# Scores' low-half products of two heads side by side on 64 rows each, the softmax of two heads at once, a permuted identity for the position adds, and the first loads spread over two queues

## The chip, the core and the metric

The kernel runs on one core of one Trainium2 chip. The metric is the device time of one execution in microseconds (us). Beside it stands one profiled execution, whose trace is read below. The engines are called as in the profile: PE multiplies matrices, PEld is its loading of weights, DVE, ACT and POOL work on vectors, SP issues most of the transfers.

## The reference

One decoder block on 512 positions of 1024 channels, cut to what the change touches:

```python
h = rms_norm(x, norm_pre)
proj = h @ w_in                       # q, keys and values of three branches, gates, retention, merge gates
# mixer A, 8 heads in 2 groups of 64 channels: compressed, selected and sliding branch
blocks = kv[tok_idx] + pe             # compress_blocks: 32 positions every 16, plus a position term
kc = gelu(flat @ w1) @ w2             # the same for the values
s = einsum('qghd,kgd->qghk', q, k) * scale
p = masked_softmax(s, mask)           # s minus its row maximum, exp, divided by the row's sum
o = g0 * o_cmp + g1 * o_sel + g2 * o_win          # o_branch = p @ v, g = sigmoid(gate)
# mixer B: retention in chunks of 128, 4 heads; then
merged = sigmoid(m_a) * y_a + sigmoid(m_b) * y_b
x = x + rms_norm(merged @ w_out, norm_post)
```

With 512 positions, 8 blocks of 64 and 16 picked blocks, the selected branch sees every earlier position, as the sliding one does, so both are plain causal attention.

## The kernel before

Every product is made of values split in two: a high half of fewer bits and a low half with the rest. A product of two split operands is three matmuls, high by high, low by high, high by low. `hTh` and `hTl` are the two halves of the scaled input, `whi` and `wlo` those of the weights, which stream from memory through four `raw` tiles and are split by ACT or DVE (`splitter`; the high half is a copy, the low half the subtraction that the profile shows as `wlo<-raw,whi`).

PE's order is written by a planner in the kernel (class `Order`): tasks are generators, each operation has an estimated cost, and the planner issues the next instruction of the task that is ready first. The main task is the row of products with the streamed weights; the tails of each product and the attention are spawned tasks that fill in. The order on each engine is fixed when the program is built.

The stages: the first product (`main`, keys and values, eight 128-row slices of the input times four tiles `t` of 128 positions), then the compressed branch's operands and the queries, the hidden layer of the compression, and the other products in the order of `PLAN`, with the attention in between.

- **First loads.** `gp` (the 8 columns of `norm_pre`) comes on ACT's queue, then the first half of the first `raw` tile, also on ACT's queue; SP's queue starts with the first slice of the transposed input (`load_xT(0)`), then the second half of that tile. Eight matmuls with `ident` keep PE busy in the meantime (line 1268). `h_split` (ACT) and `h_low` (DVE) make `hTh` and `hTl`.
- **Position adds.** `tail_a` transposes the keys and values of the compressed branch (line 226, `ident`) and adds the position term while it scatters them into `Xk` and `Xv` (line 201, `arena_f<-bank,cst`, 64 partitions): four adds for each tile `t`, whose innermost run is over 16 positions.
- **Scores.** `qT[t]` holds for each head the high half of the query in 64 rows and the low half in the other 64; `kA` the high half of the keys in both, `kB` their low half in both. One head's scores are two matmuls over all 128 rows:

```python
mm(sv, q, kA[:, b0:b0 + nb, g, 0:L], True, False)
e = mm(sv, q, kB[:, b0:b0 + nb, g, 0:L], False, True)
```

  `L` is 128(t+1), `nb` the number of branches in one task: both for t of 0 and 1, one for 2 and 3. `PS` is a ring of two PSUM banks (`bank2`, `bank3`), one for each head's scores.
- **Softmax.** For each head and branch: mask and row minimum of the negated scores on DVE (line 790, with a read of its accumulator), `Exp` on ACT with the row's sum, the reciprocal on DVE (line 218), and the scaling by reciprocal and gate: on DVE in one instruction (line 210), or on ACT if the planner's clock finds that sooner. `att_unit` and `att_block` then transpose, split and multiply by the values once the four heads of a group are done.

Of the kernel before, what the change touches and what calls it, by code (L numbers as in the profile page):

```python
# [37 lines left out]
WAKE = 8  # L38
# [3 lines left out]
class Order:  # L42
# [5 lines left out]
    def __init__(self):  # L48
        self.now = 0.0
        self.eng = {"act": 0.0, "dve": 0.0, "pool": 0.0, "dma": 0.0}  # L50
        self.ring = 500.0
        self.flying = [0.0] * 8
        self.port = 0.0
        self.exact = False
        self.cos, self.n = [], 0
        self.flags = set()
# [81 lines left out]
def block_kernel(ctx: ExitStack, tc, x, xT, g_pre, ws, small, w2s, norm_post, rope_r, dmask, out):  # L138
# [9 lines left out]
    rp = ctx.enter_context(tc.tile_pool(name="raw", bufs=1))  # L148
    pp = ctx.enter_context(tc.tile_pool(name="ps", bufs=1, space=PSUM))
# [71 lines left out]
    def mm(ps, a, b, start, stop, r=0.0, cost=None):  # L221
        T.matmul(ps, a, b, start=start, stop=stop)  # L222
        return od.pe(cost or max(0.4418 * size(b) + 1, 107 if a.shape[-1] > 64 else 54), r, a.dtype == FT)

    def tr(ps, a, idn, r=0.0):
        T.transpose(ps, a, idn)  # L226
        return od.pe(58 if a.dtype == FR else 107, r, a.dtype == FT)
# [9 lines left out]

    ident = cp.tile([P, P], FT, name="ident")
# [66 lines left out]
    def queue(i, j):  # L305

        return S if i + j == 0 else DMA

    def load_next():
        i = len(raws)  # L310
        if i < len(loads):
            raw = rp.tile([P, 1024], FT, name="raw", tag="raw", bufs=NR)
            o, c, r = loads[i][0], 0, parts[2 * (i - NR) + 1][2] if i >= NR else 0.0
            for j, n in enumerate(loads[i][1]):
                queue(i, j).dma_start(raw[:, c:c + n], ws[o:o + P * n].rearrange("(p n) -> p n", p=P))
                e = od.dma(P * n * 4, r)
                o, c = o + P * n, c + n
            raws.append((raw, e))
# [9 lines left out]
    def splitter():  # L328
        for i, (_, pieces) in enumerate(loads):
            n = sum(pieces)  # L330
            for k in range(2):
# [17 lines left out]
                e = cp_any(vh, src, r)  # L349
# [69 lines left out]
    gp = cp.tile([P, KD], FT, name="gp")  # L419
# [3 lines left out]
    rsrow = bp.tile([P, SEQ], FT, name="rsrow")  # L423
# [3 lines left out]
    def load_xT(k):  # L427
        DMA.dma_start(xTf[k], xT[k * P:(k + 1) * P, :])
        xTr[k] = od.dma(P * SEQ * 4)
# [6 lines left out]
    def h_split():  # L436
        for k in range(KD):
            yield lambda: xTr[k] > 0
            yield xTr[k], "act"
            g = gp[:, k:k + 1]  # L440
            e = act(hTh[:, k, :], xTf[k], r=xTr[k], scale=g)
            od.spawn(h_low(k, e), 0)

    def h_low(k, e):
        yield e, "dve"
        hready[k] = stt(hTl[:, k, :], xTf[k], gp[:, k:k + 1], f(hTh[:, k, :]), OP.mult, OP.subtract, e)
# [89 lines left out]
    def tail_a(t, ps, e, ring):  # L536
# [15 lines left out]
        for i in range(4):  # L552
            ep = tr(pc[:, i * P:(i + 1) * P], kd[:, i * P:(i + 1) * P], ident, e)
        KD6.put(kd, ep)
        yield ep, "dve"
        for i, X in enumerate((Xk, Xv)):
            src = pc[:, i * 256:(i + 1) * 256].rearrange("p (g c l) -> p g c l", g=2, c=8)
            for hf in range(2):
# [132 lines left out]
    def tail_q(t, ps, e):  # L691
# [6 lines left out]
        qs = qT[t].rearrange("p h (s c) -> p h s c", s=2)  # L698
        qv = qn.rearrange("p (h c) -> p h c", h=8)
        e = act(qs[:, :, 0, :], qv, r=e)  # L700
        yield e, "dve"
        e = sub_split(qs[:, :, 1, :], qv, qs[:, :, 0, :], e)
        NAT.put(qn, e)
        for g in range(2):
            pt = yield from PT.get()
            yield e + PE_LAG
            for j in range(4):
                ep = tr(pt.bitcast(FR)[:, j * P:(j + 1) * P],
                        qs[:, g * 4 + j].rearrange("p a b -> p (a b)"), identr, e)
# [65 lines left out]
    def att_head(t, g, brs, j, slot):  # L775

        L, nb, h, b0 = P * (t + 1), len(brs), g * 4 + j, brs[0]
        s = yield from PS.get()
        sv = s[:, 0:nb * L].rearrange("p (b c) -> p b c", b=nb)
        q = qT[t][:, h, :]  # L780
# [4 lines left out]
        Pj = slot["P"]  # L785
        pv = Pj[:, 0:nb * L].rearrange("p (b c) -> p b c", b=nb)
        stat = sp.tile([P, 6], FT, name="stat", tag="stat", bufs=12)
        nm, z, rz = (stat[:, 2 * i:2 * i + 2] for i in range(3))
        for b in range(nb):
            V.tensor_tensor_reduce(pv[:, b, :], sv[:, b, :], maskp[:, 512 - L:512], 1.0, -NEG, OP.add, OP.min,  # L790
                                   nm[:, b:b + 1])
            od.op("dve", 1.04 * L + 80, e)
        e = od.op("dve", 80)
        PS.put(s, e)
        yield e, "act"
        for b in range(nb):
            e = act(pv[:, b, :], pv[:, b, :], AF.Exp, r=e, bias=nm[:, b:b + 1], scale=-1.0, accum_out=z[:, b:b + 1])
        yield e, "dve"
        e = recip(rz[:, 0:nb], z[:, 0:nb], e)
        gc = h * 3 + 1 + b0  # L800
        if max(od.eng["act"], e) + (0.833 * L + 186) * nb + 190 < max(od.eng["dve"], e) + (0.521 * L + 191) * nb:
            e = tt(rz[:, 0:nb], rz[:, 0:nb], gate[:, t, gc:gc + nb], OP.mult, e)
            yield e, "act"
            for b in range(nb):
                e = act(pv[:, b, :], pv[:, b, :], r=e, scale=rz[:, b:b + 1])
        else:
            for b in range(nb):
# [572 lines left out]
```

## Time and profile before

| | |
|---|---|
| time, median of 3 runs | 532.64 us (531.42 to 532.94) |
| the profiled execution's own time | 531.09 us |
| its span, first to last instruction | 529.2 us |
| PE / PEld / DVE / ACT busy | 518.8 / 436.1 / 390.4 / 256.5 us |
| granted TensorE clock, mean | 0.998 |
| matmuls recorded | 2636 |

A matmul's end is modelled in the trace, so its duration holds the tail in which the next one already runs: what PE needs for one is read from the distance of starts, and PE's share of 98% does not say that it never waited. Where PE waited is seen at its weight loads.

### The profile page before, as it was taken

To read this page: it belongs to the slowest core of one execution; us is meant where nothing else is said; L and a number is where in the kernel's file an instruction comes from. 1 tells how busy PE (TensorE), PEld (TensorE's weight loads), DVE (VectorE), ACT (ScalarE), POOL (GpSimd) and SP (SyncE) were. 2 spreads that over 40 slices of the span, in tenths; PEclk is the share of its full clock that TensorE was granted. 3 is DMA by queue.
4 is the path that set the end of the run, shared out by engine and by line. 5 is a ranking of instruction groups with operands and counts; after the bars stand their busy time and mean duration, and the time that the engine had idled before them with its cause. 6 is when DMAs were issued, how large, how long until landed. Compare 5 with 4: busy or idle time off the path is not lost.

```text
span 529.2 us, 7325 instructions
## 1 busy us (share of the span) xinstructions
PE 518.8 (98%) x2636; PEld 436.1 (82%) x2636; DVE 390.4 (74%) x924; ACT 256.5 (48%) x552; POOL 12.9 (2%) x32
## 2 busy tenths in 40 slices
PE   8998999999999999999999999999999999999995
PEld 7896888888788888888888888888888888888885
DVE  6799799899999989997777886777737235345533
ACT  6673589448365785483546253525304224123411
POOL 1000000000000000000010000000000000000000
PEclk9999999999999999999999999999999999999999
DMA  8931127401304013123401441131814033305022
GB/s 327 382 121 54 46 66 239 175 1 40 121 1 130 31 40 117 43 84 115 146 35 41 139 142 58 41 120 40 311 48 159 18 142 125 115 1 159 1 98 101
DMA packets 18131, 55.18 MB, mean 104 GB/s; under 512 B 2096, under 2 KB 3120, under 8 KB 18096
## 3 DMA queue, kind: packets, MB, share of 16 engines
q1 hardware_dynamic: 17808, 54.46, 30.4%
q8 instruction: 20, 0.33, 0.3%
q10 hardware_dynamic: 288, 0.27, 0.2%
q14 instruction: 15, 0.12, 0.1%
HBM read 52.63 MB, written 2.10 MB: 103 GB/s over the span
## 4 chain that ended last, share of the span: by engine, by line
PE 84%; DVE 11%; issue 2%; ACT 2%; DMA 1%; DVEq 0%; POOLq 0%; POOL 0%; ACTq 0%
PE bank L222 79%; PE bank L226 5%; DVE arena_f L201 3%; DVE wlo L201 3%; DVE arena_r L201 2%; DVE arena_f L790 1%; DMA raw<-in_stream_dram 1%; DVE nat L201 1%; ACT arena_r L189 1%; ACT whi L189 1%; DVE arena_f L511 1%; DVE arena_f L210 0%; DVE arena_f L214 0%; ACT nat L189 0%; ACT arena_f L189 0%
## 5 line engine op out<-in xcount | busy, mean ns | idle before, releaser
L189 ACT ACTIVATE whi<-raw 128x512 fp32r<-128x512 f32 x151 | 91.9, 628 | 51.4 <-PE bank L222 42.0
L201 DVE TENSOR_TENSOR wlo<-raw,whi 128x512 fp32r<-128x512 f32 x160 | 102.9, 686 | 3.9 <-ACT whi L189 3.3
L222 PE MATMUL bank<-whi,hTh 128*128 128x512 f32 x256 | 99.4, 404 | 0.9 <-ACT whi L189 0.9
L222 PE MATMUL bank<-wlo,hTh 128*128 128x512 f32 x256 | 96.3, 391 | 0.1
L222 PE MATMUL bank<-whi,hTl 128*128 128x512 f32 x256 | 96.3, 391 | 0.0
L222 PE MATMUL bank<-arena_r 128*128 128x256 f32 (+2 forms) x328 | 70.3, 335 | 0.0
L189 ACT ACTIVATE arena_r<-bank 128x512 fp32r<-128x512 f32 (+2 forms) x80 | 45.1, 570 | 46.5 <-PE bank L226 46.3
L222 PE MATMUL bank<-hTh,whi 128*128 128x512 f32 x160 | 63.4, 396 | 0.0
L222 PE MATMUL bank<-hTh,wlo 128*128 128x512 f32 x160 | 62.6, 391 | 0.2 <-DVE wlo L201 0.2
L222 PE MATMUL bank<-hTl,whi 128*128 128x512 f32 x160 | 62.5, 390 | 0.0
L222 PE MATMUL bank<-arena_r,whi 128*128 128x512 f32 x192 | 59.2, 389 | 0.0
L222 PEld LDWEIGHTS bank<-whi,hTl 128*128 128x128 f32 x256 | 48.1, 188 | 10.5
L222 PEld LDWEIGHTS bank<-arena_r 128*128 128x128 f32 x328 | 50.8, 190 | 6.3 <-DVE stat L790 0.3
L222 PEld LDWEIGHTS bank<-whi,hTh 128*128 128x128 f32 x256 | 48.0, 188 | 9.2 <-ACT whi L189 1.0
L222 PEld LDWEIGHTS bank<-wlo,hTh 128*128 128x128 f32 x256 | 48.2, 188 | 9.0 <-DVE wlo L201 0.5
L201 DVE TENSOR_TENSOR arena_r<-bank,arena_r 128x512 fp32r<-128x512 f32 (+2 forms) x72 | 46.9, 656 | 8.3 <-ACT arena_r L189 7.6
L222 PE MATMUL bank<-whi,arena_r 128*128 128x512 f32 (+1 forms) x176 | 49.0, 353 | 0.0
L222 PEld LDWEIGHTS bank<-arena_r,whi 128*128 128x128 f32 x192 | 36.0, 188 | 7.6 <-DVE sg L214 0.2
L189 ACT ACTIVATE arena_f<-arena_f,stat 128x512 f32<-128x512 f32 (+3 forms) x64 | 35.3, 555 | 11.3 <-DVE stat L790 11.2
L226 PE MATMUL bank<-ident,arena_f 128*128 128x128 f32 (+1 forms) x260 | 38.5, 274 | 1.6 <-DVE arena_f L511 1.0
L226 PEld LDWEIGHTS bank<-ident,arena_f 128*128 128x128 f32 (+1 forms) x260 | 31.0, 138 | 9.9 <-DVE arena_f L511 1.5
L222 PE MATMUL bank<-arena_r,wlo 128*128 128x512 f32 x96 | 37.3, 389 | 0.0
(117 smaller groups left out, 669.6 us busy)
## 6 DMA issues: line engine op xcount, KB each, us to landing
raw<-in_stream_dram SPq DMA_DIRECT2D x79, 512.0 KB, 4.1
arena_f<-in_x_dram SPq DMA_DIRECT2D x8, 512.0 KB, 6.9
arena_f<-in_xT_dram SPq DMA_DIRECT2D x8, 256.0 KB, 5.8
arena_f<-in_rope_r_dram SPq DMA_DIRECT2D x8, 256.0 KB, 2.5
out_dram<-arena_f SPq DMA_DIRECT2D x6, 256.0 KB, 2.0
raw<-in_stream_dram SPq DMA_DIRECT2D x4, 280.0 KB, 7.1
arena_f<-in_norm_post_dram SPq DMA_DIRECT2D x1, 512.0 KB, 7.9
out_dram<-arena_f SPq DMA_DIRECT2D x2, 192.0 KB, 1.9
```

The lines of the kernel that those rows point to most:

```text
L189: S.activation(o, i, func, **kw)
L201: (V if e == "dve" else G).tensor_tensor(o, a, b, op=op)
L222: T.matmul(ps, a, b, start=start, stop=stop)
L226: T.transpose(ps, a, idn)
L511: V.tensor_copy(kd.rearrange("p (a r c) -> p a r c", a=n, r=2), kn[:, a:b].rearrange("p (a c) -> p a c", c=64).unsqueeze(2).broadcast_to([ ...
L790: V.tensor_tensor_reduce(pv[:, b, :], sv[:, b, :], maskp[:, 512 - L:512], 1.0, -NEG, OP.add, OP.min, nm[:, b:b + 1])
```

## The change

- Scores: `att_head` becomes `att_pair`, for two heads. Both heads' first products (`kA`) stay as they are; the second ones (`kB`) use only the 64 rows in which the query's high half stands, rows 0 to 63 for the first head and 64 to 127 for the second. For that, `tail_q` puts the low half first in every second head. The product of the two low halves, which was part of the second matmul, is left out. A pair takes both banks of `PS` at once.
- Softmax: the two heads share `stat`; one reciprocal serves both. The rule that picks the engine for the scaling is another (the sum on ACT's side no longer carries 190, DVE's side gets 1000 more), and on ACT's side one small product of reciprocals and gates goes ahead.
- Positions: the transposes of the compressed branch take `identp`, `ident` with its columns permuted, so that the result stands position by position, and the adds run over 8 or 7 blocks innermost.
- Start: `x0` holds `norm_pre` and the first 256 columns of the first input slice and comes on ACT's queue; SP's queue begins with the first half of the first `raw` tile, then the other 256 columns, then the second half. The first `whi` is always cast by DVE. The matmuls at the start are seven, on a zeroed `rsrow`.
- Planner: other estimated costs for matmuls and transposes.

```diff
-    def pe(self, cost, r=0.0, exact=False):
-        if exact != self.exact:
-            cost += 100.0 if exact else 85.0
-            self.exact = exact
+    def pe(self, cost, r=0.0, after=0.0):
+        cost += 0.0 if after else self.after
+        self.after = after
...
-        return od.pe(cost or max(0.4418 * size(b) + 1, 107 if a.shape[-1] > 64 else 54), r, a.dtype == FT)
+        return od.pe(cost or (0.4418 * size(b) + 2 if size(b) > 64 else 112 if a.shape[-1] > 64 else 54), r)
...
+    identp = ep.tile([P, P], FT, name="identp")
+    V.tensor_copy(identp.rearrange("p (l c) -> p l c", l=16), ident.rearrange("p (c l) -> p l c", l=16))
...
-                e = cp_any(vh, src, r)
+                if p:
+                    e = cp_any(vh, src, r)
+                else:
+                    V.tensor_copy(vh, src)
+                    e = od.op("dve", copy_ns(vh, src), r, True)
...
-            ep = tr(pc[:, i * P:(i + 1) * P], kd[:, i * P:(i + 1) * P], ident, e)
+            ep = tr(pc[:, i * P:(i + 1) * P], kd[:, i * P:(i + 1) * P], identp, e)
...
-                o = X[rr, :, :, c0 + lo:c0 + 8].rearrange("p l g c -> p g c l")
-                ep = tt(o, src[rr, :, lo:8, :],
-                        pes[i][rr, :].unsqueeze(1).unsqueeze(1).broadcast_to([64, 2, 8 - lo, 16]), OP.add, ep)
+                o = X[rr, :, :, c0 + lo:c0 + 8].rearrange("p l g c -> p g l c")
+                ep = tt(o, src[rr, :, :, lo:8],
+                        pes[i][rr, :].unsqueeze(1).unsqueeze(3).broadcast_to([64, 2, 16, 8 - lo]), OP.add, ep)
...
-    def att_head(t, g, brs, j, slot):
-        s = yield from PS.get()
-        mm(sv, q, kA[:, b0:b0 + nb, g, 0:L], True, False)
-        e = mm(sv, q, kB[:, b0:b0 + nb, g, 0:L], False, True)
+    def att_pair(t, g, brs, j, slots):
+        yield lambda: len(PS.free) >= 2
+        for i in range(2):
+            mm(sv[i], qT[t][:, h + i, :], kA[:, b0:b0 + nb, g, 0:L], True, False)
+        for i in range(2):
+            r = slice(i * 64, i * 64 + 64)
+            e = mm(sv[i], qT[t][r, h + i, :], kB[r, b0:b0 + nb, g, 0:L], False, True, cost=15 if i else None)
...
-        if max(od.eng["act"], e) + (0.833 * L + 186) * nb + 190 < max(od.eng["dve"], e) + (0.521 * L + 191) * nb:
+        if max(od.eng["act"], e) + (0.833 * L + 186) * 2 * nb < max(od.eng["dve"], e) + (0.521 * L + 191) * 2 * nb + 1000:
...
-    S.dma_start(gp, g_pre)
-    load_xT(0)
+    S.dma_start(x0, x0s)
     load_next()
...
-        T.matmul(banks[0][:, 0:P], ident, ident, start=True, stop=True)
+        T.matmul(banks[0][:, 0:P], rsrow[:, 0:P], rsrow[:, 0:P], start=True, stop=True)
```

What this makes of the order, at three places. First PE, where the attention of the last tile (t = 3) begins; `bank2` and `bank3` take scores, `bank0` the query product, `identr` marks the transposes of the queries. Before:

```order
L226 MATMUL bank5_86<-identr_94,arena_r_80 128x128 x4
L222 MATMUL bank2_83<-arena_r_80 128x512 x2
L226 MATMUL bank4_85<-identr_94,arena_r_80 128x128 x4
L222 MATMUL bank3_84<-arena_r_80 128x512 x2
L222 MATMUL bank0_81<-whi_414,hTh_98 128x512
L222 MATMUL bank0_81<-wlo_415,hTh_98 128x512
```

After the change:

```order
L222 MATMUL bank2_86<-arena_r_83 128x512
L222 MATMUL bank3_87<-arena_r_83 128x512
L222 MATMUL bank2_86<-arena_r_83 128x512
L222 MATMUL bank3_87<-arena_r_83 128x512
L226 MATMUL bank5_89<-identr_99,arena_r_83 128x128 x4
L222 MATMUL bank0_84<-whi_371,hTh_105 128x512
```

Two heads' four matmuls now stand together, the last two of them on 64 rows each; there are 24 such pairs, 12 with 512 columns, 8 with 384 and 4 with 256. In the program the number of matmuls stays the same but for the one fewer at the start.

Second DVE, at the first scores (line 790 before and 809 after are the masked minimum; the second row of each is the read of its accumulator). Before:

```order
L790 ISA arena_f_79,stat_738<-bank3_84,maskp_113 128x512
L790 ISA stat_738 128x1
L218 RECIPROCAL stat_733<-stat_733 128x1
L210 TENSOR_SCALAR arena_f_79<-arena_f_79,stat_733,gate_115 128x512
L790 ISA arena_f_79,stat_761<-bank2_83,maskp_113 128x512
```

After the change:

```order
L809 ISA arena_f_82,stat_750<-bank3_87,maskp_119 128x512
L809 ISA stat_750 128x1
L218 RECIPROCAL stat_750<-stat_750 128x2
L201 TENSOR_TENSOR stat_750<-stat_750,gate_121 128x2
L809 ISA arena_f_82,stat_771<-bank2_86,maskp_119 128x512
```

The scaling (line 210) is gone from DVE here. In the whole program 58 of the 64 scalings move to ACT (14 of 512 columns, 16 of 384, 16 of 256, 12 of 128), 48 reciprocals become 24, 22 small products with the gates are new, and 7 more copies of `whi` stand on DVE in place of ACT.

Third SP's queue at the start, before:

```order
L428 DMA arena_f<-in_xT_dram 128x512
L315 DMA raw<-in_stream_dram 128x512
L428 DMA arena_f<-in_xT_dram 128x512 x2
L315 DMA raw<-in_stream_dram 128x1024
```

After the change:

```order
L315 DMA raw<-in_stream_dram 128x512
L435 DMA arena_f<-in_xT_dram 128x256
L315 DMA raw<-in_stream_dram 128x512
L435 DMA arena_f<-in_xT_dram 128x512 x2
```

The first half of the first `raw` tile has moved from ACT's queue, where it stood second, to the head of SP's; the rest follows in the same sequence as before.

## Rows read from the trace of the kernel before

**Rows 1.** Parts of the page: busy time of each engine (share, instructions), the clock granted to PE in 40 slices, and the chain of work that ended last by engine.

```profile
PE 518.8 (98%) x2636; PEld 436.1 (82%) x2636; DVE 390.4 (74%) x924; ACT 256.5 (48%) x552; POOL 12.9 (2%) x32
...
PEclk9999999999999999999999999999999999999999
...
PE 84%; DVE 11%; issue 2%; ACT 2%; DMA 1%; DVEq 0%; POOLq 0%; POOL 0%; ACTq 0%
```

**Rows 2.** Busy time by stretch: the stretch, its length, then busy time (instructions) of PE, PEld, DVE, ACT and POOL, the granted clock, the transfers' share and GB/s.

```profile
27.00:56.00 29.00, 27.18 (x172) 23.32 (x171) 28.04 (x88) 14.70 (x39) 0.94 (x4) 1.00 0.26 88
56.00:100.00 44.00, 43.83 (x261) 37.17 (x260) 39.02 (x101) 34.12 (x76) 0.00 (x0) 1.00 0.43 145
100.00:150.00 50.00, 49.90 (x264) 41.54 (x264) 47.05 (x118) 27.54 (x64) 0.00 (x0) 1.00 0.15 48
150.00:200.00 50.00, 49.98 (x263) 42.02 (x261) 45.64 (x129) 34.62 (x85) 0.00 (x0) 1.00 0.16 53
200.00:250.00 50.00, 49.91 (x252) 41.27 (x251) 45.96 (x134) 27.19 (x73) 0.00 (x0) 1.00 0.30 95
```

**Rows 3.** The chain of work from 365 us on: start, length, what (x pieces).

```profile
365.32 0.44 PE bank L226 x4
365.76 152.53 PE bank L222 x676
```

**Rows 4.** What PE's weight loads waited for, from 27 to 56 us and from 56 to 365 us: engine, line, releaser, total us, times, longest.

```profile
PEld bank L226 <- DVE arena_f L511: 1.5, 2, 0.9
PEld bank L226 <- DVE arena_r L201: 1.2, 3, 0.8
PEld bank L226 <- DVE arena_f L201: 0.7, 1, 0.7
...
PEld bank L222 <- DVE wlo L201: 1.3, 3, 0.6
PEld bank L222 <- DVE stat L790: 0.8, 3, 0.5
PEld bank L222 <- DVE arena_r L201: 0.7, 2, 0.4
```

**Rows 5.** The start in order of time: start, length, engine (ACTq and SPq are the queues), line, operation, count, and in brackets the idle time before and its releaser.

```profile
0.72 0.40 ACTq L1261 DMA_DIRECT2D gp<-in_norm_pre_dram  x1
...
0.73 0.37 SPq L428 DMA_DIRECT2D arena_f<-in_xT_dram  x1
...
1.16 0.45 ACTq L315 DMA_DIRECT2D raw<-in_stream_dram  x1
...
3.64 0.72 ACT L189 ACTIVATE hTh<-arena_f,gp 128x512 fp32r<-128x512 f32 x1 [0.50 <-DMA gp<-in_norm_pre_dram]
...
5.14 0.63 ACT L189 ACTIVATE whi<-raw 128x512 fp32r<-128x512 f32 x1 [0.78 <-DMA raw<-in_stream_dram]
...
5.82 1.19 PE L222 MATMUL bank<-whi,hTh 128*128 128x512 f32 x4 [0.86 <-ACT whi L189]
...
8.12 1.15 ACT L189 ACTIVATE whi<-raw 128x512 fp32r<-128x512 f32 x2 [0.52 <-DMA raw<-in_stream_dram]
...
8.68 1.07 PE L222 MATMUL bank<-whi,hTh 128*128 128x512 f32 x4
...
11.40 1.07 PE L222 MATMUL bank<-whi,hTh 128*128 128x512 f32 x4
...
13.21 1.07 PE L222 MATMUL bank<-wlo,hTh 128*128 128x512 f32 x4
```

**Rows 6.** From issue to landing (us) of the first input slice on SP's queue (line 428, to 1.2 us).

```profile
DMA to landing us min/median/max: 2.7/2.7/2.7
```

**Rows 7.** PE around a group of transposes, in order of time (columns as in rows 5).

```profile
99.39 0.60 PE L226 MATMUL bank<-ident,arena_f 128*128 128x128 f32 x4
99.75 1.17 PE L222 MATMUL bank<-arena_r 128*128 128x512 f32 x4
100.75 0.39 PE L222 MATMUL bank<-hTh,whi 128*128 128x512 f32 x1
```

**Rows 8.** Groups of instructions of one form over the whole span: line, engine, operation, tiles and shapes, count | busy us, mean ns of one | idle time before and releasers.

```profile
L222 PE MATMUL bank<-whi,hTl 128*128 128x512 f32 x256 | 96.3, 391 | 0.0
...
L222 PEld LDWEIGHTS bank<-arena_r 128*128 128x128 f32 x328 | 50.8, 190 | 6.3 <-DVE stat L790 0.3
...
L189 ACT ACTIVATE arena_f<-arena_f,stat 128x512 f32<-128x512 f32 x16 | 11.4, 717 | 3.2 <-DVE stat L790 3.1
L790 DVE CUSTOM_DVE_ANT_0 arena_f<-bank,maskp 128x512 f32<-128x512 f32 x16 | 10.8, 686 | 0.0
...
L210 DVE TENSOR_SCALAR arena_f<-arena_f,stat,gate 128x512 f32<-128x512 f32 x16 | 8.8, 547 | 0.6
...
L201 DVE TENSOR_TENSOR arena_f<-bank,cst 64x256 f32<-64x256 f32 x14 | 8.6, 615 | 0.2
...
L201 DVE TENSOR_TENSOR arena_f<-bank,arena_f 128x256 f32<-128x256 f32 x14 | 5.9, 422 | 2.1 <-ACT arena_f L189 1.9
```

**Rows 9.** The same for all softmax instructions that touch `stat`, forms together: operation, count, duration ns least/median/most.

```profile
L189 ACT ACTIVATE arena_f<-arena_f,stat x64: 384/555/731, 63.3 to 245.9; 128x512 f32<-128x512 f32 x16, 128x384 f32<-128x384 f32 x16, 128x256 f32<-128x256 f32 x16, 128x128 f32<-128x128 f32 x16
...
L210 DVE TENSOR_SCALAR arena_f<-arena_f,stat,gate x64: 339/448/551, 64.4 to 248.5; 128x512 f32<-128x512 f32 x16, 128x384 f32<-128x384 f32 x16, 128x256 f32<-128x256 f32 x16, 128x128 f32<-128x128 f32 x16
L218 DVE RECIPROCAL stat<-stat x48: 145/156/166, 64.2 to 248.1; 128x1 f32<-128x1 f32 x32, 128x2 f32<-128x2 f32 x16
```

More of the change, by code (lines that the diff above doesn't have):

```diff
@@ L53, in __init__ @@
         self.port = 0.0
-        self.exact = False
+        self.after = 0.0
         self.cos, self.n = [], 0
@@ L137, in block_kernel @@
 @with_exitstack
-def block_kernel(ctx: ExitStack, tc, x, xT, g_pre, ws, small, w2s, norm_post, rope_r, dmask, out):
+def block_kernel(ctx: ExitStack, tc, x, xT, x0s, ws, small, w2s, norm_post, rope_r, dmask, out):
     nc = tc.nc
@@ L314, in load_next @@
             for j, n in enumerate(loads[i][1]):
-                queue(i, j).dma_start(raw[:, c:c + n], ws[o:o + P * n].rearrange("(p n) -> p n", p=P))
+                DMA.dma_start(raw[:, c:c + n], ws[o:o + P * n].rearrange("(p n) -> p n", p=P))
                 e = od.dma(P * n * 4, r)
                 o, c = o + P * n, c + n
+                if i + j == 0:
+                    load_xT(0)
             raws.append((raw, e))
@@ L438, in h_split, with h_parts @@
             yield lambda: xTr[k] > 0
[L439 to L441 removed]
+            for c, v in h_parts(k):
+                yield xTr[k], "act"
+                e = act(hTh[:, k, c], v, r=xTr[k], scale=gp[:, k:k + 1])
             od.spawn(h_low(k, e), 0)
+    def h_parts(k):
+        return ((slice(0, 256), x0[:, KD:KD + 256]), (slice(256, 512), xTf[0][:, 256:512])) if k == 0 else ((slice(0, 512), xTf[k]),)
     def h_low(k, e):
[L445 to L446 removed]
+        for c, v in h_parts(k):
+            yield e, "dve"
+            hready[k] = stt(hTl[:, k, c], v, gp[:, k:k + 1], f(hTh[:, k, c]), OP.mult, OP.subtract, e)
         od.flags.add(f"h{k}")
@@ new lines, in att_pair @@
+        yield lambda: len(PS.free) >= 2
+        ss_ = []
+        for _ in range(2):
+            ss_.append((yield from PS.get()))
+        sv = [s[:, 0:nb * L].rearrange("p (b c) -> p b c", b=nb) for s in ss_]
+        for i in range(2):
[3 more added lines that the diff above has]
+            e = mm(sv[i], qT[t][r, h + i, :], kB[r, b0:b0 + nb, g, 0:L], False, True, cost=15 if i else None)
@@ new lines, in att_pair @@
+        stat = sp.tile([P, 3, 2, 2], FT, name="stat", tag="stat", bufs=6)
+        nm, z, rz = (stat[:, k, :, 0:nb] for k in range(3))
+        pv = [s["P"][:, 0:nb * L].rearrange("p (b c) -> p b c", b=nb) for s in slots]
+        em = []
+        for i in range(2):
+            yield e, "dve"
+            for b in range(nb):
+                V.tensor_tensor_reduce(pv[i][:, b, :], sv[i][:, b, :], maskp[:, 512 - L:512], 1.0, -NEG, OP.add, OP.min,
+                                       nm[:, i, b:b + 1])
+                em.append(od.op("dve", 1.04 * L + 85, e))
+            PS.put(ss_[i], em[-1])
@@ L811, in att_block @@
     def att_block(t, g, br, b, kt, slots, lastblk):
+        yield lambda: "po" in avs[t, g] and all("r" in s for s in slots)
         r = max(s["r"] for s in slots)
-        yield lambda: "po" in avs[t, g]
         yield r + PE_LAG
@@ L845, in attention @@
                     slots = []
-                    for j in range(4):
-                        s = {"P": (yield from PR.get())}
-                        slots.append(s)
-                        od.spawn(att_head(t, g, brs, j, s), 3)
+                    for j in (0, 2):
+                        for _ in range(2):
+                            slots.append({"P": (yield from PR.get())})
+                        od.spawn(att_pair(t, g, brs, j, slots[j:j + 2]), 3)
                         yield
@@ L1363 @@
     add("xT", x.T)
[L1364 removed]
+    add("x0", np.concatenate([np.asarray(inputs["norm_pre"]).reshape(KD, P).T, x.T[0:P, 0:256]], axis=1))
     rope_n, rope_r, dmask = _tables()
```

74 lines of the change are left out of this document (34 added, 40 removed).

## The prediction

> **What bounds the kernel now.** I read the page first: PE is busy 98% of the span, the chain that ended last is PE for 84%, and the granted clock is at its upper level (2.4 GHz) in every slice [rows 1]. So what counts is PE's own work and the places where PE stands still. The reader should not take the 98% at its word: a 512-column matmul is shown with 0.391 us [rows 8], but from 8.68 to 13.21 us twenty start in 4.53 us, 0.2265 us each [rows 5], that is 0.4424 ns a column. The last third has this rhythm without a break, 152.53 us for 676 matmuls, 0.2256 each [rows 3], and the change touches nothing there.
>
> Then I asked where PE waits. From 27 to 56 us its weight loads stand for DVE, 1.5 + 1.2 + 0.7 = 3.4 us in the three largest groups; from 56 to 365 us the three groups ended by DVE make 1.3 + 0.8 + 0.7 = 2.8 us [rows 4]. DVE is the reason: 28.04 of 29 us busy in the first stretch, and 39.02 + 47.05 + 45.64 + 45.96 = 177.7 of 194 us from 56 to 250, while ACT has 34.12 + 27.54 + 34.62 + 27.19 = 123.5 there [rows 2]. At the start PE waits for the first weights until 5.82 us [rows 5]. So there is PE work to be taken away, about 6 us of waits for DVE, and the start.
>
> **A. The start.** Before, the first `raw` half stands second on ACT's queue, and ACT can cast it from 5.14 us [rows 5]. Now it stands first on SP's queue, where the first input slice stood: the same 256 KB, issued at 0.73 [rows 5] and landed 2.7 later [rows 6], at 3.43 us. DVE has nothing else to do then and casts it in about 0.4 (estimate: a scaling of 512 columns on DVE takes 0.547 [rows 8]), so `whi` is there near 3.9. The other operand is now the later one. `x0` is 135 KB at the place where 4 KB of `gp` let ACT begin at 3.64 [rows 5]; half of the 1.5 us that the next 256 KB on that queue took (3.64 to 5.14) more gives 4.4, and a half-width ACT copy about 0.5 (below the 0.72 of the full one [rows 5]): 4.9 us. PE gains 5.82 - 4.9 = 0.9. If `x0` lands at once it is 1.7; if it lands as late as the `raw` half did, 5.14 + 0.5, it is 0.2. I take **-0.9**, between the ends. It lasts: the third slice's `whi` is begun at 8.12 and finished at 9.27, and PE takes it up at 11.40 [rows 5], 2 us of room. The zeroing, the permuted identity and the seven matmuls on zeros stand before the first data and cost nothing, unless the clock is still at its lower level (1.2 GHz) at 4.9 us: then the first slice's 12 matmuls take up to 12 x 0.23 = 2.7 more, which would use up the term.
>
> **B. The scores.** The second products of two heads run on 64 rows each. If both run at once, 12 x 512 + 8 x 384 + 4 x 256 = 10,240 columns are no longer streamed: 10,240 x 0.4424 ns = -4.53 us. What a second product still costs is not in this trace, since nothing in it works on a part of the rows. Below it is nothing; above it is all of the 4.53, if the two do not run at once. The nearest row is the least step between two starts: 99.39 to 99.75 holds four transposes [rows 7], three steps of 0.11 [rows 3] leave 0.03. 24 x 0.03 = +0.7. The array also changes shape 48 times, into 64 rows and back. The nearest row for a change of kind is transposes to plain matmuls: 99.39 to 100.75 us [rows 7] is 1.36, less 4 x 0.11 and 4 x 0.2265, which leaves about 0.01 for two changes. The other end is that PE runs empty at each change: what a matmul takes beyond its step, 0.391 - 0.2265 = 0.16 us, 48 times, 7.9 us. I take the row that is a change on PE itself, 48 x 0.01 = +0.5. Sum **-3.3**.
>
> The Trainium skill speaks against this: "TensorEngine Tiling (Array Packing)", Tiling Modes, says that a change of tiling mode drains TensorE. No run here shows it yet; by that page the 7.9 us above would stand in place of my 0.5, and it is the first rival below. The skill's "TensorE: Matmul & The Clock Gate", Part 3, has concurrent tiles starting some 4 ns apart; by it my 0.7 would be 0.1.
>
> **C. The position adds.** Sixteen adds into scattered places, 14 of 0.615 us [rows 8] and two a little shorter, some 9.7 us. With the permutation both reading and writing go along runs of 8; an add of as many values out of a bank takes 0.422 [rows 8], so up to 16 x 0.19 = 3.0 us less on DVE; at the other end runs of 8 cost what runs of 16 in scattered order did, and nothing changes. DVE is without a break in this stretch, so all of it comes forward, but PE can win no more than its waits for DVE, 3.4 us in weight loads, some of which lie under running matmuls. I take two thirds, **-2.3** (0 to -3.0).
>
> **D. The softmax.** DVE loses 58 scalings, 58 x 0.448 = 26.0 us by the median of all [rows 9], and 24 reciprocals of 0.156 = 3.7 [rows 9]; it gains 22 small products (like a reciprocal, 3.4) and 7 copies of about 0.4 (2.9). Net -23 us of 177.7 in 56 to 250. ACT gains 58 x 0.555 = 32.2 [rows 9] less the 7 copies: about +28 on 123.5, of 194. Neither is full on average. What PE can win here is its 2.8 us of waits for DVE; since DVE falls from 92% to 80%, I take less than half, **-1.2**. Ends: -2.8, and a loss through ACT (second rival).
>
> **Sum.** -0.9 - 3.3 - 2.3 - 1.2 = -7.7. The profiled execution took 531.09 us (span 529.2 and 1.9 around it), so 523.4. It lies 1.55 under the median of the runs shown; the forecast for a median is 532.64 - 7.7 = **524.9 us**. Less than 0.3% (1.6 us) can't be told from no change in this kernel, whose three runs spread over 1.5 us.
>
> **Rivals.**
>
> *PE runs empty at each change of shape.* Place: both sides of each of the 24 pairs. For it: PE's tail of 0.16 us is in every row, and a matmul in another shape may have to wait for it. Against it: transposes and plain matmuls pass each other for 0.01. Then B is -4.5 + 0.7 + 7.9 = +4.1 and the total -0.3: 532.3, no change. If moreover the two halves run one after the other, as matmuls of one shape do everywhere in this trace, B is +7.9, the total +3.5, and the time **536 us, slower**. With halves one after the other, the gain of the other terms (4.4) is gone at 4.4/48 = 0.09 us a change, and slower by more than the bound from (4.4 + 1.6)/48 = 0.125 on.
>
> *Half a gain in the pairs.* The second half's weights (0.190 us [rows 8]) are loaded only when the first half streams, so it starts about 0.16 late: 24 x 0.16 = +3.8 in place of 0.7. Total -4.6: 528. The chain would show PE's second halves 0.1 to 0.2 apart.
>
> *ACT becomes the bound.* From 56 to 100 us ACT is busy 34.1 of 44 us [rows 2], and the 14 wide scalings at 0.717 [rows 8] add 10.0: 44.1 of 44. It is behind ACT that `whi` and the copies out of the banks stand, and PE behind these. If half of the 10 lands on PE, D is +5.0 in place of -1.2: total -1.5, 531. Against it: attention may spread, since ACT has 22 us free from 100 to 150.
>
> *Banks.* A pair needs both score banks, so PE can't write the next pair until DVE has read both: 2 x 0.686 [rows 8] and the accumulator reads, 1.5 us, where before one bank freed half of it. The built order puts other matmuls between pairs, and few gaps are under 2 us; six waits of 0.5 are +3: 528.
>
> **How the numbers follow.** Forecast 0.54 (own range 521.5 to 527.5); half a gain 0.12; banks 0.10; ACT 0.10; empty array without change 0.08, with slower 0.06. The first three and a little of the fourth are faster: 0.80; the rest of ACT and the empty array within 0.3%: 0.13; slower 0.07. The range of 8 in 10 goes from 520.5 (the starts of all terms: A 1.4, B 4.5, C 3.0, D 2.8 give 11.7, 520.9) up to 531.5, which leaves out only the empty array.
>
> **What would show it.** A: the first product matmul near 4.9 us. B: the two 64-row matmuls start 0.03 us apart, and the next full one about 0.23 after them for 512 columns; 0.16 more on either side is the empty array. C: the adds at 0.42, and the waits for DVE from 27 to 56 us mostly gone. D: DVE about 23 us less, ACT 28 more, no new waits of PE for ACT between 56 and 100 us. The end, 366 us on, keeps its length. I am wrong if 64-row matmuls are not side by side, or if ACT's new work reaches PE.

## The result and the profile after

The changed kernel takes 537.06 us (median of four executions, 536.5 to 537.35) against 532.79 before (531.42 to 533.39): ratio 1.0087, interval 1.0064 to 1.0109. By the ratio it is 4.6 us slower; the forecast was 7.7 us faster. The profiled execution took 536.5 us (span 534.7), 5.4 us more than the profiled execution of before. In some executions PE takes about double the time for its first 12 matmuls (rows in the last section), so medians of few executions can lie some 2 us apart; smaller differences are read from the ratios and their intervals. The expectations below call DVE VectorE and PE TensorE.

Parts of the page of after, to be read against [rows 1].

```profile
PE 523.2 (98%) x2634; PEld 433.5 (81%) x2634; DVE 369.3 (69%) x874; ACT 277.7 (52%) x604; POOL 12.6 (2%) x32
...
PEclk9989999999999999999999999999999999999998
...
PE 90%; DMA 4%; DVE 3%; issue 1%; SPq 0%; ACT 0%; POOLq 0%; DVEq 0%; POOL 0%
```

DVE lost 21.1 us of work, 3.0 of them in the adds (9.7 us before, 6.7 after), and ACT gained 21.2. The forecast had 23 for DVE without the adds, and 28 for ACT: the work moved, about a quarter less of it. Neither bought time: PE has 4.4 us more busy time though 10,240 fewer columns pass one after the other, the third slice of the clock shows less than full speed, and transfers have 4% of the chain instead of 1%.

Busy time by stretch in after (columns and stretches as [rows 2], the first row 26 to 36 us).

```profile
26.00:36.00 10.00, 7.50 (x45) 7.14 (x44) 9.45 (x35) 7.85 (x19) 0.23 (x1) 0.83 0.78 266
27.00:56.00 29.00, 26.50 (x169) 24.36 (x169) 26.20 (x87) 15.48 (x41) 0.95 (x4) 0.94 0.31 107
56.00:100.00 44.00, 42.40 (x246) 33.85 (x245) 36.84 (x96) 33.05 (x71) 0.00 (x0) 1.00 0.42 130
100.00:150.00 50.00, 50.00 (x261) 39.57 (x260) 41.24 (x105) 34.34 (x75) 0.00 (x0) 1.00 0.18 60
150.00:200.00 50.00, 50.00 (x253) 39.14 (x252) 36.74 (x111) 40.20 (x100) 0.00 (x0) 1.00 0.13 43
200.00:250.00 50.00, 50.00 (x257) 40.89 (x256) 45.40 (x125) 36.86 (x103) 0.00 (x0) 1.00 0.35 111
```

The reader should see three things. From 26 to 36 us PE is busy 7.50 of 10 and its granted clock falls to 0.83. From 56 to 100 it stands 1.6 us, where it stood 0.17. From 150 to 200 us PE is at 50.00 of 50 and issues 253 instructions, where before it issued 263. The mix of widths differs a little, so this only hints that a PE that looks busy gets less done; the rows of one pair below show it.

The chain of after at the end (as [rows 3]).

```profile
371.12 152.55 PE bank L222 x676
```

The last run of 676 matmuls is as long as before and starts 5.36 us later (365.76 in [rows 3]). All of the loss lies ahead of it.

### A pair of heads in after

PE and its weight loads around one pair, from 65.85 us (columns as in [rows 5]; x4 are the two full products and the two halves).

```profile
65.85 1.06 PE L222 MATMUL bank<-arena_r 128*128 128x512 f32 x4
65.86 0.19 PEld L222 LDWEIGHTS bank<-arena_r 128*128 128x128 f32 x1
66.41 0.19 PEld L222 LDWEIGHTS bank<-arena_r 64*128 64x128 f32 x2 [0.36 <-issue]
...
66.84 0.19 PEld L222 LDWEIGHTS bank<-whi,hTh 128*128 128x128 f32 x1 [0.25 <-issue]
66.84 0.50 PE L222 MATMUL bank<-whi,hTh 128*128 128x512 f32 x1
...
66.95 0.19 PEld L222 LDWEIGHTS bank<-wlo,hTh 128*128 128x128 f32 x1
67.18 0.40 PE L222 MATMUL bank<-wlo,hTh 128*128 128x512 f32 x1
```

The two halves' weights lie in one row, 0.19 us for both: the halves do run side by side. But the four matmuls hold the engine from 65.85 to 66.84, 0.99 us, where three steps of 0.2265 and 0.03 would be 0.71; and the next step, 66.84 to 67.18, is 0.34 instead of 0.23. That is 0.39 us over the working of the forecast. Read in the same way, all 24 pairs lie near it, whatever their width: 0.41 on average, 24 x 0.41 = 9.8 us. The loads say where: a weight load here normally starts one step ahead of its matmul (66.95 for the matmul at 67.18), while that of the halves comes after 0.36 us idle, and that of the next full matmul starts in the same hundredth as the matmul itself, after 0.25 idle. Over the whole span this wait is 9.6 us.

Waits of the weight loads of line 222 in after.

```profile
PEld bank L222 <- issue: 9.6, 35, 0.4
```

### The profile page after: what moved, and what is told of

Read it like the earlier page. It is cut to its first block, busy times and chain, and to the rows that moved or that the text cites. A ratio compares the mean times of both kernels' runs of the same rounds, so it can differ in the third digit from the quotient of the medians.

```text
span 534.7 us, 7345 instructions
## 1 busy us (share of the span) xinstructions
PE 523.2 (98%) x2634; PEld 433.5 (81%) x2634; DVE 369.3 (69%) x874; ACT 277.7 (52%) x604; POOL 12.6 (2%) x32
## 4 chain that ended last, share of the span: by engine, by line
PE 90%; DMA 4%; DVE 3%; issue 1%; SPq 0%; ACT 0%; POOLq 0%; DVEq 0%; POOL 0%
PE bank L222 84%; PE bank L226 7%; DMA raw<-in_stream_dram 4%; DVE wlo L201 1%; DVE arena_r L201 0%; DVE whi L197 0%; DVE arena_f L201 0%; SPq L435 0%; DVE arena_f L214 0%; SPq L315 0%; ACT nat L189 0%; DVE arena_f L809 0%; ACT whi L189 0%; ACT arena_r L189 0%; POOLq L1398 0%
## 5 line engine op out<-in xcount | busy, mean ns | idle before, releaser
L189 ACT ACTIVATE whi<-raw 128x512 fp32r<-128x512 f32 x144 | 86.2, 627 | 52.9 <-PE bank L222 44.8
L222 PE MATMUL bank<-whi,hTh 128*128 128x512 f32 x256 | 100.6, 408 | 0.3 <-ACT hTh L189 0.3
L222 PE MATMUL bank<-arena_r 128*128 128x256 f32 (+5 forms) x328 | 68.2, 350 | 0.0
L189 ACT ACTIVATE arena_f<-arena_f,stat 128x384 f32<-128x384 f32 (+3 forms) x122 | 63.5, 557 | 3.9 <-DVE stat L201 3.0
L222 PE MATMUL bank<-hTh,whi 128*128 128x512 f32 x160 | 64.7, 405 | 0.0
L222 PEld LDWEIGHTS bank<-arena_r 128*128 128x128 f32 (+1 forms) x328 | 47.0, 188 | 11.9 <-issue 6.5
L222 PEld LDWEIGHTS bank<-whi,hTh 128*128 128x128 f32 x256 | 48.1, 188 | 10.5 <-issue 1.2
L226 PE MATMUL bank<-ident,arena_f 128*128 128x128 f32 (+1 forms) x244 | 37.3, 276 | 2.5 <-DVE arena_f L522 2.5
L226 PEld LDWEIGHTS bank<-ident,arena_f 128*128 128x128 f32 (+1 forms) x244 | 29.4, 139 | 9.4 <-issue 2.9
```

Of the source, the lines that this page charges most:

```text
L189: S.activation(o, i, func, **kw)
```

## The experiments

Two theories went in. **Theory 1**: going into 64 rows and back costs about 0.41 us a pair (the mean over the three widths), more than the columns that it saves; the halves do run at once. **Theory 2**: the halves are cheap and save their 4.5 us, and the loss comes from the other parts, the first loads and the softmax. The edits keep the order on every engine, or leave it to the planner where the text says so.

**e1_full_rows**: after, with the second products on all 128 rows.

```
-            r = slice(i * 64, i * 64 + 64)
+            r = slice(0, 128)
```

> The changed kernel with one edit: the second score products take all 128 rows again, in the order and with the planner's costs of the changed kernel, so that every engine's order is the same. Theory 1 (each pair pays for the change into the 64-row shape and back): the trace of the changed kernel shows 0.41 us of extra steps around each of the 24 pairs against 4.5 us of saved columns, so without the shape the time falls by about 24 x 0.41 - 4.5 = 5.3 us, to 531.5 to 532.5. Theory 2 (the 64-row halves gain, and the new order of attention, with two banks per pair and scaling on ACT, loses): the time rises by 4 to 4.5 us, to about 541.

Measured 530.55 us, ratio to before 0.9975 (0.9958 to 0.9993). Theory 2 falls: without the halves the kernel is some 6 us faster than after, in the same order. The pair of the rows above, in e1:

```profile
66.21 0.88 PEld L222 LDWEIGHTS bank<-arena_r 128*128 128x128 f32 x4
...
66.44 1.07 PE L222 MATMUL bank<-arena_r 128*128 128x512 f32 x4
...
67.13 0.19 PEld L222 LDWEIGHTS bank<-whi,hTh 128*128 128x128 f32 x1
67.35 0.39 PE L222 MATMUL bank<-whi,hTh 128*128 128x512 f32 x1
67.58 0.39 PE L222 MATMUL bank<-wlo,hTh 128*128 128x512 f32 x1
```

Four full matmuls take 0.91 us and the next step is 0.23; every load starts a step ahead. So four full ones are 0.08 + 0.11 = 0.19 us shorter than two full ones and two halves.

**e2_same_rows**: after, with both halves on rows 0 to 63, so that they can't run at once.

```
-        qh, ql = qs[:, :, 0:4:3, :], qs[:, :, 1:3, :]
+        qh, ql = qs[:, :, 0:4:2, :], qs[:, :, 1:4:2, :]
-            r = slice(i * 64, i * 64 + 64)
+            r = slice(0, 64)
```

> The changed kernel with both second products of a pair on rows 0 to 63 (every head's high half stands there, as before the change), the order otherwise held. Theory 1: the changes of shape are the same 48, but the two halves run one after the other, so the time rises by the 4.5 us of columns, to about 541.5, and the starts of the two stand 0.23 us apart for 512 columns; if the second one's weights can't be loaded under the first, 24 x 0.1 to 0.2 more, up to 546. Theory 2: the same 4.5 us. If the halves did not really run at once in the changed kernel, nothing changes: 537.

Measured 539.59 us, ratio 1.0145 (1.0115 to 1.0174). A pair in e2:

```profile
64.29 1.28 PE L222 MATMUL bank<-arena_r 128*128 128x512 f32 x4
64.84 0.29 PEld L222 LDWEIGHTS bank<-arena_r 64*128 64x128 f32 x2 [0.36 <-issue]
65.50 0.50 PE L222 MATMUL bank<-whi,hTh 128*128 128x512 f32 x1
```

1.21 us instead of 0.99: just one step of 0.2265 more. This confirms that the halves of after run at once. The rows also part the price. From the first full product to the first half, 64.29 to 64.84, are two steps and 0.10 us; from there to the next full product are two steps and 0.21, of which the trace has 0.11 between the two halves, where no change lies, and 0.10 ahead of the full one. So each change costs 0.10 ahead of its first product, and 0.11 on the step behind that product. The kernel is 2.5 us over after by the medians (3.1 by the ratios, two executions) rather than the 4.5 of its columns; the profiled e2 kept its clock at 26 to 36 us, where after lost it.

**e3_before_half**: before, with only the second products on 64 rows (one head at a time).

```
-        e = mm(sv, q, kB[:, b0:b0 + nb, g, 0:L], False, True)
+        e = mm(sv, q[0:64], kB[0:64, b0:b0 + nb, g, 0:L], False, True)
```

> The kernel before with one edit: each head's second score product takes rows 0 to 63 alone, so the product of the low halves is left out; every engine's order is the same, and nothing runs side by side. It prices the change of shape by itself: 48 heads, 96 changes. Theory 1: 48 x 0.41 = 19.7 us more, about 552. Theory 2 (a change of shape costs little, 0.01 us): 533, no change.

Measured 548.84 us, ratio 1.0319 (1.0282 to 1.0355): 16.5 / 48 = 0.34 us a head, with no column saved and every order kept; the product of the two low halves is left out. That is less than the 0.41 expected; why is not shown. Weight loads and matmuls of two heads in e3:

```profile
61.28 1.67 PE L222 MATMUL bank<-arena_r 128*128 128x512 f32 x4
...
61.60 0.18 PEld L222 LDWEIGHTS bank<-arena_r 64*128 64x128 f32 x1 [0.36 <-issue]
62.02 0.19 PEld L222 LDWEIGHTS bank<-arena_r 128*128 128x128 f32 x1 [0.24 <-issue]
62.45 0.18 PEld L222 LDWEIGHTS bank<-arena_r 64*128 64x128 f32 x1 [0.24 <-issue]
62.88 0.19 PEld L222 LDWEIGHTS bank<-whi,hTh 128*128 128x128 f32 x1 [0.24 <-issue]
62.88 0.50 PE L222 MATMUL bank<-whi,hTh 128*128 128x512 f32 x1
```

Between changes the loads come 0.43 us apart, a step of 0.23 and 0.20 more, and none is ahead of its matmul. Theory 1 stands in the main: the change of shape is dear by itself.

**e4_full_replanned**: e1, with the planner told the full cost of both second products, so that it orders anew.

```
-            e = mm(sv[i], qT[t][r, h + i, :], kB[r, b0:b0 + nb, g, 0:L], False, True, cost=15 if i else None)
+            e = mm(sv[i], qT[t][r, h + i, :], kB[r, b0:b0 + nb, g, 0:L], False, True)
```

> The changed kernel with the second products on all 128 rows and their planned cost that of a full matmul, so that the order is planned anew. Theory 1: it is what the rest of the change is worth without the 64-row shape: about the first run of this call or a little better, 530 to 532.5. Theory 2: above 537.

Measured 530.57 us, ratio 0.9975 (0.9960 to 0.9991). The rest of the change brings 1.3 us, not the 4.4 of the prediction (0.9 + 2.3 + 1.2). The next runs ask which of A, C and D fell short.

**e5_before_new_start**: before, with the new first loads alone (of the diff: `x0`, the queues, the cast of the first `whi`, the wake-up).

> The kernel before with the new first loads alone (x0 with the first 256 columns, the two queues exchanged, whi's first cast on VectorE, the wake-up matmuls on zeros); the planner orders the rest anew. The record's step A says that the 0.9 us lasts: 531.5 against 532.4 of before. The rival, from the trace of after: the first product comes about 1 us earlier, but the loads, which are one transfer of 0.47 us further back in their queue and keep the 16 DMA engines busy until 26 us, give it back by 32 us: 532.4 to 533.5, so not below before.

Measured 532.46 us, ratio 1.0002 (0.9987 to 1.0017): no gain, as the rival had it. **e8_full_old_start** is e4 with the first loads of before.

> The kernel of e4 with the first loads as before (that part of the change undone); planned anew. By the record's step A it loses 0.9 us: 531.5. By the rival of e5 the loads are earlier by 0.5 us from 6 us on, the stop at 29 us is shorter, and the time is 529.5 to 530.6.

Measured 529.54 us, ratio 0.9951 (0.9932 to 0.9969), 1.3 us under e4 by the ratios. The two intervals just overlap, so the times alone hardly settle that the new loads cost something here; the stretch from 26 to 36 us shows where they do (columns as [rows 2]). In before:

```profile
26.00:36.00 10.00, 10.00 (x75) 9.69 (x74) 9.52 (x38) 9.13 (x25) 0.47 (x2) 1.00 0.51 167
```

In e8, with the old loads:

```profile
26.00:36.00 10.00, 10.00 (x75) 9.53 (x74) 9.59 (x40) 8.62 (x24) 0.47 (x2) 1.00 0.66 213
```

In e4, with the new ones:

```profile
26.00:36.00 10.00, 8.30 (x62) 7.88 (x62) 9.62 (x38) 7.99 (x22) 0.24 (x1) 1.00 0.76 265
```

With the old loads PE goes through with 75 instructions; in e4 it stands 1.7 us and issues 62. After (above) stands 2.5 us and issues only 45; there the clock falls as well.

**e6_full_old_pos**: e1, with the positions' old identity and adds.

```
-            ep = tr(pc[:, i * P:(i + 1) * P], kd[:, i * P:(i + 1) * P], identp, e)
+            ep = tr(pc[:, i * P:(i + 1) * P], kd[:, i * P:(i + 1) * P], ident, e)
...
-            src = pc[:, i * 256:(i + 1) * 256].rearrange("p (g l c) -> p g l c", g=2, l=16)
+            src = pc[:, i * 256:(i + 1) * 256].rearrange("p (g c l) -> p g c l", g=2, c=8)
```

> The kernel of e1 (128 rows) with the positions' old identity and old adds; the order on every engine is that of e1, with only these instructions changed. If step C's price lasts to the end (0.35 us less for each of eight groups of adds, about 2.3 us on the path), this takes 530.6 + 2.3 = 532.9 and the first 52 us of the trace are later than e1's by that. If the wait for the loads at 29 us swallows it, 530.5 to 531.2.

Measured 533.40 us, ratio 1.0021 (1.0003 to 1.0039), which is 2.4 us over e1: step C's price holds to the end. Its profiled execution began with doubled steps (last section), so its first 52 us can't be laid beside e1's.

**e7_full_rate345**: e4, with the planner's rate for loads lowered.

```
-            self.eng["dma"] = max(self.eng["dma"], self.ring + 625) + nbytes / n / 380.0
+            self.eng["dma"] = max(self.eng["dma"], self.ring + 625) + nbytes / n / 345.0
```

> The kernel of e4 (128 rows, planned anew) with one number of the planner changed: it assumes 345 bytes per ns for the loads, not 380, and so puts VectorE's rotations ahead of the low halves that wait for late loads. If the stop of 1.7 to 2.9 us at 29 us comes of VectorE's order behind loads that are later than planned, it shrinks below 0.8 us and the time is 528.8 to 529.6. If it comes of the loads themselves, TensorE waits for wlo instead, and the time stays at 530.6.

Measured 530.83 us, ratio 0.9976 (0.9964 to 0.9987): no better than e4. Inconclusive on the stop: the profiled execution began with doubled steps (last section) and so came 2 us late to the place where the loads are missing, and found them there.

**e9_softmax_alone**: e8 with e6's edit. Of the change the new softmax is left, with the pairing of heads that goes with it, and also the planner's new estimates. **e10_halves_old_start**: e8 with the halves (e1's edit reversed), so the change without its loads. **e11_best_rate345**: e8 with e7's edit.

> The kernel of e8 with the positions' old identity and adds, in e8's order: of the whole change only the softmax of two heads at once, with its grouping of the score products, is left. By the record's step D (1.2 us) it takes 532.7 - 1.2 = 531.5. By what e6 and e8 leave over (e8 is 3.2 us under before, of which the adds are 2.5) it takes 531.8 to 532.4, because the wait for VectorE that it saves behind 150 us comes back at 67 to 80 us.

> The kernel of e8 with the second products in 64 rows each again, two of a pair side by side, in e8's order on every engine: the change with its first loads undone. If a pair costs 0.41 us by the change of shape and saves 0.19 of columns, and this is all that parts e1 from after, it takes 529.6 + 6.5 = 536.1. If part of those 6.5 us came of the later loads, that the new start brings, it takes under 534.

> The kernel of e8 with the planner's rate for loads at 345 bytes per ns instead of 380. With the old first loads there is no stop at 29 us that this could shorten, so the order moves for nothing: 529.5, and within 1 us to either side by what else the new order moves. If e7's stop of 1.3 to 2.4 us at 70 to 75 us comes with this rate, 530.5.

Measured: e9 532.88 us, ratio 0.9999 (0.9985 to 1.0013): the softmax with the new estimates brings nothing. No run parts the two. e10 534.11 us, ratio 1.0038 (1.0023 to 1.0053): the halves cost 0.0087, 4.6 us, over e8, a little less than between e1 and after (0.0112, 6.0 us), and after lies 0.0049, 2.6 us, over e10, the price of its loads (and of its order, which is not e10's; but e1 and e4, which differ in the order alone, have the same ratio). The expectation of 536.1 was too high by 2, and 534.11 lies just above the 534 under which part of the 6.5 was to come of the loads. e11 531.78 us, ratio 0.9986 (0.9969 to 1.0002): 1.9 us over e8 by the ratios, where no change was expected. The new order costs; why was not followed up, but the lower rate gains nothing with either start.

**e12_adds_alone**: before, with the permuted identity and the new adds alone, in the order of before.

> The kernel before with the permuted identity and the new adds alone, in the order of before. By the record's step C, and by e8 against e9, the adds are worth 2.3 to 2.6 us to the end: 530.0. If they are worth that much only where the new softmax lets the gain through, 531 to 532.5.

Measured 528.47 us, ratio 0.9935 (0.9914 to 0.9957): the lowest of all, by the ratios 3.5 us under before and 8.1 under the whole change. Busy time of e12 from 27 to 56 us (columns as [rows 2]):

```profile
27.00:56.00 29.00, 29.00 (x190) 25.82 (x188) 27.22 (x96) 16.29 (x44) 0.95 (x4) 1.00 0.31 99
```

PE has no gap left (before 27.18 of 29, 172 instructions [rows 2]).

## Why the prediction was wrong, point by point

**B, the failed step: "I take the row that is a change on PE itself, 48 x 0.01 = +0.5".** The row was that of transposes beside plain matmuls [rows 7], which both use 128 rows and columns; a change into 64 rows measured another price. The sum had the saved columns (4.5) and the halves at once right; the 48 changes cost 4.5 + 4.6 = 9.1 us by e10 against e8, 4.5 + 6.0 = 10.5 by after against e1, that is about 0.4 us a pair in place of 0.02. The clock that fell with the stop is in the profiles of after and e1 and not in those of e8 and e10 (1.00 from 26 to 36 us), so 4.6 is the cleaner figure; the 9.8 us added up from the rows, less 4.5, give 5.3. The term was +4.6 to +6.0 in place of -3.3. This alone brings the sum from -7.7 to between +0.2 and +1.6, so the gain is gone. With the 4.6, the rest of the way to the measured +4.6 is A (+2.6 for -0.9) and D (+0.9 for -1.2), less the 1.2 that C gave beyond its forecast. The first rival had the mechanism and named 0.16 us a change, 7.9 in all: near, and still too low, and I gave it 0.14 in two parts. It said "0.16 more on either side"; the rows have 0.10 before the halves, 0.20 behind them and 0.11 on the step after that. The Trainium skill, "TensorEngine Tiling (Array Packing)", Tiling Modes, says that a change of tiling mode drains TensorE. The rows go with it: no weight load runs ahead across the change. By e2 the 0.20 behind the halves is two parts, 0.11 on the step behind the first change and 0.10 ahead of the second. The 0.11 can be read at the loads: after the change that of the second product starts at 66.95, 0.11 behind the first product's at 66.84, and its matmul comes its usual 0.23 later. Why each change costs 0.10 ahead of its first product, the array running empty or something else, is not shown.

**A: right at its place, wrong on "It lasts".** Start of after:

```profile
3.96 0.43 DVE L354 CAST whi<-raw 128x512 fp32r<-128x512 f32 x1 [2.00 <-DMA raw<-in_stream_dram]
...
4.17 0.51 ACT L189 ACTIVATE hTh<-x 128x256 fp32r<-128x256 f32 x1 [1.50 <-DMA x<-in_x_dram]
...
4.73 1.28 PE L222 MATMUL bank<-whi,hTh 128*128 128x512 f32 x4 [0.33 <-ACT hTh L189]
```

The first product comes at 4.73 us, 1.09 earlier than in [rows 5] (forecast 0.9). I looked for room at the third slice and found 2 us; I should have looked where the loads run out. The chain of waits in after (start, length, what) goes through a transfer there:

```profile
19.09 6.99 DMA raw<-in_stream_dram
```

DVE and PE of after in order of time, behind that transfer:

```profile
26.18 0.43 DVE L197 CAST whi<-raw 128x512 fp32r<-128x512 f32 x1 [0.29 <-DMA raw<-in_stream_dram]
...
26.88 1.93 DVE L201 TENSOR_TENSOR wlo<-raw,whi 128x512 fp32r<-128x512 f32 x3
28.87 0.43 DVE L197 CAST whi<-raw 128x512 fp32r<-128x512 f32 x1
29.21 1.89 DVE L201 TENSOR_TENSOR wlo<-raw,whi 128x512 fp32r<-128x512 f32 x3
31.02 0.42 DVE L201 TENSOR_TENSOR arena_f<-nat,cst 128x64 f32<-128x64 f32 x3
...
32.44 0.66 PE L226 MATMUL bank<-ident,arena_f 128*128 128x128 f32 x2 [2.50 <-DVE arena_f L522]
```

DVE of before at the same work:

```profile
24.76 0.43 DVE L197 CAST whi<-raw 128x512 fp32r<-128x512 f32 x1 [0.90 <-DMA raw<-in_stream_dram]
...
25.46 2.49 DVE L201 TENSOR_TENSOR wlo<-raw,whi 128x512 fp32r<-128x512 f32 x4
28.02 0.43 DVE L201 TENSOR_TENSOR arena_f<-nat,cst 128x64 f32<-128x64 f32 x3
```

The rotation (`arena_f<-nat,cst`) that PE's transposes need starts at 31.02 instead of 28.02. The cast waits for its load until 26.18 instead of 24.76, which is 1.4 of the 3.0 us; the rest is work in between, six low halves and a second cast where before four low halves stood. One reason for the later load is at the head of SP's queue, one transfer more: the second `raw` piece is issued at 1.63 us instead of 1.16, 0.47 later, while the transfers' share from 4 us on stays between 0.89 and 1.03 until 26 us in both kernels. How 0.47 grows to 1.4 is not shown. PE is still 1.0 us ahead when its products of 280 columns begin (26.71 against 27.72), so the 1.1 us were lent, and the stop of 2.5 took them back and more. The lower clock behind it takes some 1.7 more (0.17 of 10 us, an estimate from the row of 26 to 36 us). A is 0 by e5, +1.3 by e4 against e8 (about as much as its interval) and +2.6 by after against e10, in place of -0.9; together: no gain, and a loss whose size the runs don't settle.

**C: right, if anything too small.** The adds take what was read for them, and e8 against e9 (0.0048, 2.6 us), e6 against e1 (2.4) and e12 against before (3.5) put the term at 2.4 to 3.5 for a forecast of 2.3. The form of [rows 8] in after:

```profile
L201 DVE TENSOR_TENSOR arena_f<-bank,cst 64x256 f32<-64x256 f32 x14 | 5.9, 422 | 1.2 <-PE bank L226 1.0
```

0.422 us, the value of the row that I had taken as the near one. In after the adds are as fast, but the stop at 29 us lies in the same stretch and takes as much (PE 26.50 of 29 there, before 27.18).

**D: nothing instead of -1.2.** That is e9, 0 with 0.7 us to either side, for the softmax and the planner's estimates together. Part of the term came: behind 100 us the weight loads' waits for DVE fell from 1.7 us in before (0.8 + 0.5 + 0.4) to 0.6 in e8 (0.4 + 0.2). But new waits stand ahead of it. Busy time from 76 to 86 us (columns as [rows 2]) in e8:

```profile
76.00:86.00 10.00, 9.42 (x69) 8.47 (x68) 9.63 (x21) 10.00 (x21) 0.00 (x0) 1.00 0.74 244
```

And in e12, whose softmax is the old one:

```profile
76.00:86.00 10.00, 10.00 (x77) 9.25 (x76) 9.96 (x20) 9.38 (x21) 0.00 (x0) 1.00 0.66 227
```

ACT is full, DVE is still at 9.63, and PE stands 0.58. From 56 to 100 us PE stands 1.7 us in e8, where it stood 0.17 before, and ACT has 37.24 us of 44 there against 34.12 [rows 2]. PE's waits end at DVE, but ACT stands behind DVE: of the chain of waits from 66 to 92 us ACT's three largest lines hold 52% in e8 and 17% in e12. This is the ACT rival on a small scale. In after ACT has 33.05, its lines hold little of that chain, and PE waits for DVE. Waits of PE in after from 56 to 100 us (line, releaser, total us, times, longest):

```profile
PE bank L222 <- DVE wlo L201: 1.0, 2, 0.6
PE bank L226 <- DVE arena_r L201: 0.6, 1, 0.6
```

DVE has 17.5 us less work from 56 to 250 us, and 15.3 of them lie behind 100, where PE was busy 49.90 to 49.98 of 50 already [rows 2]. The prediction read the mean share (92% to 80%) and not the stretch.

**The other rivals.** Half a gain in the pairs and waits for the score banks did not come: the halves' weights lie in one row, no wait of PE or of its loads in after ends at line 809, which reads the score banks, and PE has 50.00 of 50 in the three stretches from 100 to 250 us. The rival of 536 us came nearest to the measured time, but by chance: in it the halves run one after the other, and they don't. The cases that were to make the kernel faster held 0.80; all of them shared the price of the change of shape, so they were one bet and not four.

**The split as the runs have it**, step by step from before by differences of ratios: adds -3.5 (e12), softmax with the planner's estimates +0.9 (e8 against e12, within the intervals nothing), halves +4.6 (e10 against e8), loads +2.6 (after against e10). Only the adds came as forecast.

## What to carry to other kernels

A cost that no row of the trace shows should not be priced by the row that only looks alike: a transpose is a change of operation, 64 rows are a change of the array's shape. Where the sum turns on such a term, its dear end deserves as much weight as the cheap one. Here two changes, 0.4 us, stood against 0.19 us of saved columns on average and 0.23 at the most (512 columns), so a single pair between full products can't win; whether longer runs of 64-row products would pay, no run here tried. The earlier start was worth nothing here because the loads set the pace some 25 us on: look for the next place where the data is short before counting it; and time taken from a busy engine counts only in the stretch where it is waited for.

## What the runs showed of the hardware

*Shape.* Between products of 128 and 64 rows weights are not loaded ahead (rows of after and e3). In after the steps grow by 0.10 us into the halves, 0.20 out of them and 0.11 behind that; by e2 this is 0.10 ahead of the first product of each shape and 0.11 on the step behind it.

*The clock at a stop.* With stops of 2.3 to 2.9 us at 29 us the granted clock from 26 to 36 us is 0.83 or 0.84, a mixture of its two levels (1.2 and 2.4 GHz), in after, e1 and e5; with the stop of 1.7 us in e4 and e2 it is 1.00. From 12 us up to the stop PE was busy without a gap in after, e1, e4 and e5.

*The first matmuls.* In the profiled e6, e7, e9 and e11 the products of the first slice, 12 matmuls, take about twice as long. PE's first products in e9, four to a row:

```profile
5.76 2.08 PE L222 MATMUL bank<-whi,hTh 128*128 128x512 f32 x4 [0.62 <-ACT whi L189]
7.63 1.91 PE L222 MATMUL bank<-whi,hTl 128*128 128x512 f32 x4
9.34 1.78 PE L222 MATMUL bank<-wlo,hTh 128*128 128x512 f32 x4
```

And in e8, whose code differs from e9's in the adds alone:

```profile
5.76 1.19 PE L222 MATMUL bank<-whi,hTh 128*128 128x512 f32 x4 [0.75 <-ACT whi L189]
```

From 7.63 to 9.34 the steps in e9 are 0.43 us, about twice the 0.23 elsewhere, which is the lower level, 1.2 GHz. The view's granted clock reads 1.00 from 4 to 12 us in both, but the trace's own record of the clock begins only at 10.84 us in e9 and at 4.75 in e8, and the view counts the time ahead of it as full speed; the doubled steps end where the record begins. The first product starts at the same 5.76 us in both, so the kernel's order doesn't decide it. The Trainium skill, "TensorE: Matmul & The Clock Gate", Part 1, says that the number of slow matmuls at the start differs from run to run of one kernel. The profiles here go with it, though each is of another kernel: twelve in these four, three in e2, none in e8 and e4. Why it falls so in one execution and not in another stays open.
